# First gated features of the down projection loaded through the weights' rings in the last pair, with the A12 product behind the sixth product

## The chip, the cores and the metric

The program runs on one core of one Trainium2 chip. The metric is the device time of one execution in microseconds. The engines that matter here are TensorE (PE, matmuls), VectorE (DVE), ScalarE (ACT), GpSimd (POOL) and SyncE (SP), which issues all DMAs of this part of the program. Each engine works through its own instructions in program order; an instruction waits until the semaphores it needs have been raised.

## What is computed

Two layers of a hybrid block over 1024 latent tokens and 256 context tokens, each a mixing part and a channel part. The change lies in the channel part, which in both layers runs over the latent tokens with 1024 model features and 2816 hidden features:

```
def conv_ffn(h, w_up, w_conv, w_down):
    u = dwconv3(h @ w_up, w_conv)
    a, b = jnp.split(u, 2, -1)
    return (jax.nn.silu(a) * b) @ w_down

x = x + g2_x * rmsnorm(conv_ffn(hx, w_up[l], ffn_conv_w[l], w_down[l]), g_post_ffn[l])
```

`dwconv3` is a centred depthwise convolution of width 3 over the tokens. In layer 0 the context tokens take the same path afterwards.

## The kernel before

All matmuls are float32 products made of three: an operand is split into a high part (a rounded copy, `act.copy`, on ScalarE) and a low part (`dve.tensor_sub`, on VectorE), and high x high, high x low and low x high are summed.

**Up projection.** Hidden features go in 22 pairs `f` of 128 gate and 128 value features. The product of a pair, 256 features by 1024 tokens, is made as seven block products of half the size (`q1` to `q7`, 12 matmuls of 128 x 128 by 512 columns each), whose operands are sums and differences of the blocks of the weights and the tokens. `q2` is the product with the upper right block of the weights, A12, added in PSUM to `q1`'s result ("G"); `ev2` copies it out (L1191, ScalarE). `q7` and `q5` start the two halves of one PSUM tile "M2" (`cd`), `q5` ends with a copy of its half (L1204). `q6` goes to "M1"; when it is done, VectorE makes `v` (L1213) and `z` (L1214, from `v` and `q7`'s half). `q3` adds to the half that `q5` began, `q4` to that of `q7`; both write into the tile that `z` reads, and wait for `z`. On TensorE the order in a pair is `q7`, `q2`, `q5`, `q6`, `q3`, `q1` of the next pair, `q4`; the last pair has no `q1` behind it.

`gated(f)` then makes the pair's gated features: `z` and the copy of `q5` are joined (L1228), `cd` and `v` (L1226), `conv3` runs on both halves (L342 on ScalarE, L343 and L344 on VectorE), then SiLU (L1230), the product (L1232) and a write of the 128 x 1024 tile to DRAM, `gscr` (L1233). Its two tiles are from the pool "HC".

**Down projection.** When the last pair is done, the pools of the up projection close and the pool `dn` opens in their room. The tokens go in three groups of 384, 384 and 256. In each, the 22 tiles of gated features are worked off in steps of two (FG = 2; "group 0" is features 0 and 1 of the first token group, "group 1" features 2 and 3). For each feature a tile `gr` of the group's tokens is loaded from `gscr` (L1441), split into `gh` (L1443, ScalarE) and `gl` (L1444, VectorE), and multiplied with 128 rows of `w_down` (L1402 to L1404, in `down_into`). Matmuls of a group go by token tile, then by half of the output columns, then by feature: the third matmul of a group is the first that reads `gl` of its first feature, the sixth the first that reads `gl` of its second. Group 0 has 36 matmuls.

**Rings.** `weight()` loads a block into a "RAW" tile (3 buffers, L114) and splits it into "WH" and "WL" (4 buffers each; L118 on ScalarE, L119 on VectorE). The same three rings serve the up projection's weights (L1122, L1123 make their splits, and also those of the sums `s31` and `ss2`). `w_down` of features 0 and 1 (w0, w1) comes that way. `w_down` of features 2 to 9 stays resident: RAW (L1450), and a split into "H" tiles (L1452, L1453). A RAW buffer is free for the next load when its split is done.

**Beside it in layer 0.** After each group one step of the next layer's modulation runs: 1 MB of `w_mod` into an "HC" tile (L173) and 8 small matmuls (L184). And the norm of the two context tiles that come later is made early: loads of "T4" tiles (L1370), square and sum (L245, ScalarE), variance (L238, VectorE), a power (L239, GpSimd) and the scaling (L247, VectorE), once for each tile.

**What sets the order.** The program is recorded in the order of the source and then ordered anew, engine by engine, by a list scheduler with a cost for each instruction; an engine's order can thus differ from the source's. The rows of order below show what came out.

Of the kernel before, what the change touches and what calls it, by code (L numbers as in the profile page):

```python
# [6 lines left out]
F32 = mybir.dt.float32  # L7
F32R = mybir.dt.float32r
# [6 lines left out]
P = 128  # L15
# [9 lines left out]
FG = 2  # L25
# [3 lines left out]
def build(tc, d, out, dbg=None):  # L29
    nc = tc.nc  # L30
    act, dve, pool, pe, sp = nc.scalar, nc.vector, nc.gpsimd, nc.tensor, nc.sync
# [19 lines left out]
    gscr = [[dram.t([P, N], f"gscr{l}_{f}") for f in range(FF)] for l in range(DEPTH)]  # L51
# [22 lines left out]
    def M1():  # L74
        return cur["pool"].t([P, 512], "M1", cur["tags"]["M1"])
# [32 lines left out]
    def raw_tile():  # L108
        return wp.t([P, 1024], "RAW", 3)
# [768 lines left out]
    for l in range(DEPTH):  # L878
# [204 lines left out]
        def gate(s):  # L1083
            g = op.t([P, D], "gt", 1)
            gate_tile(m, 0, s, g)
            return g
# [7 lines left out]
        g, xn = None, []  # L1094
# [23 lines left out]
        def S():  # L1118
            return up_.t([P, 512], "S", 6)
# [6 lines left out]
        def wtiles():  # L1126
            return wp.t([P, 1024], "WH", 4, F32R), wp.t([P, 1024], "WL", 4, F32R)
# [57 lines left out]
        def q2(f):  # L1185
            blocks(pair[f]["a"], pair[f]["a1"], 1, b21, False)

        def ev2(f):
            w = pair[f]
            w["u"], w["w"] = hp_.t([P, 2, N], "HC", 2), hp_.t([P, 2, N], "HC", 2)  # L1190
            act.copy(w["u"][:, 0, 0:512], w["a"])  # L1191

        def q7(f, js=range(4)):
            w = pair[f]
            if js[0] == 0:
                w["cd"] = M2()
            blocks(w["cd"][:, 512:1024], w["s31"], 0, t3, True, js)
# [8 lines left out]
        def q6(f, js=range(4)):  # L1206
            w = pair[f]
            if js[0] == 0:
                w["b"] = M1()
            blocks(w["b"], w["ss2"], 1, t2, True, js)  # L1210
            if js[-1] == 3:
                w["v"], w["z"] = S(), S()
                dve.tensor_sub(w["v"], w["s1"], w["b"])  # L1213
                dve.tensor_add(w["z"], w["v"], w["cd"][:, 512:1024])  # L1214
# [28 lines left out]
        for i, t in enumerate(order):  # L1243
# [14 lines left out]
            if t == order[0] or t == 0:  # L1258
                g = gate(0 if t < NT else 1)
# [58 lines left out]
        for f in range(FF):  # L1318
            more = f + 1 < FF
            if f:  # L1320
                q7(f)
            if f and more:
                prep0(f + 1)
            if f > 1:
                q2(f)
            ev2(f)
            if f:
                q5(f)
                q6(f)
            if more:  # L1330
                prepa(f + 1)
                prepx(f + 1)
            if f:
                q3(f)
            if f and more:
                q1(f + 1)
            if more:
                prepy(f + 1)
            q4(f)
            gated(f)  # L1340
# [9 lines left out]
        dn = Pool(f"dn{l}", bufs=1, side="left")  # L1350
# [81 lines left out]
        for ts in ((0, 1, 2), (3, 4, 5), (6, 7)):  # L1432
            n0, n = P * ts[0], P * len(ts)
            pts = [M2() for _ in ts]
            xt = []
            for f0 in range(0, FF, FG):
                fs = range(f0, f0 + FG)
                g, w = {}, {}
                for f in fs:
                    gr = dn.t([P, n], "gr", 4)  # L1440
                    sp.dma_start(out=gr, in_=gscr[l][f][:, n0 : n0 + n])  # L1441
                    gh, gl = g[f] = dn.t([P, n], "gh", 6, F32R), dn.t([P, n], "gl", 6, F32R)
                    act.copy(gh, gr)  # L1443
                    dve.tensor_sub(gl, gr, gh.bitcast(F32))  # L1444
                    blk = d["w_down"][l, P * f : P * f + P, :]
                    if f in wd:
                        w[f] = wd[f]
                    elif FG <= f < FG + RES:
                        raw = raw_tile()
                        sp.dma_start(out=raw, in_=blk)  # L1450
                        h = H()
                        act.copy(h[:, 0], raw)  # L1452
                        dve.tensor_sub(h[:, 1], raw, h[:, 0].bitcast(F32))  # L1453
                        w[f] = wd[f] = h[:, 0], h[:, 1]
                    else:
                        w[f] = weight(blk)
                if f0 == FF - 3 * FG:
                    for t in ts:
                        x = dn.t([P, D], "x", 3)
                        sp.dma_start(out=x, in_=xmid[l][t])  # L1460
                        xt.append(x)
                for i, t in enumerate(ts):
                    for ns in halves:
                        for f in fs:
                            down_into(pts[i][:, ns], ns, g[f], w[f], slice(P * i, P * i + P), f == 0, f == FF - 1)
                    if f0 == FF - FG:
                        end_tile(t, pts[i], xt[i])
                for _ in range(4 if n0 == 0 else 2):
                    next(it2, None)
            if with_ctx and n0:  # L1470
                tkc = tkc or ctx_h2()
# [6 lines left out]
        if with_ctx:  # L1478
# [7 lines left out]
            g = {}  # L1486
# [124 lines left out]
```

## Time and profile before

| | us |
|---|---|
| median of 3 runs | 2774.09 (2771.47 to 2774.62) |
| profiled execution | 2772.39 |
| its span in the profile | 2770.5 |
| TensorE busy | 2677.6 (97%) |
| VectorE busy | 1712.1 (62%) |
| ScalarE busy | 1142.7 (41%) |
| GpSimd busy | 101.3 (4%) |

The mean granted clock of the execution is 0.99 of full. Busy time counts a matmul from its start to a modelled end, and matmuls overlap, so the share of TensorE doesn't tell how near it is to its peak. What is idle, and why, is read from the rows of single stretches.

### The profile page before, as it was taken

Reading aid. Unit: us, or ns where it says so; the run is one execution under the profiler, and the core shown is the slowest. Engines: PE = TensorE matmul, PEld = TensorE weight load, DVE = VectorE, ACT = ScalarE, POOL = GpSimd, SP = SyncE. Lnnn points to the kernel's source line nnn. Section 1 sums busy time; section 2 is a strip of 40 time slices with the busy share of each in tenths; the row PEclk is TensorE's granted clock in tenths of the full one; section 3 lists DMA queues with packets and bytes.
Section 4 is the critical chain, followed back from the end, with each engine's and each line's share of the span. In section 5 each row is a group of like instructions: output and inputs, shape, how many; then the busy total and the mean of one; then the engine's idle time right before and its main releaser. Section 6 shows DMA issues by size and latency. Waiting matters only on the chain. (4 is left out here: it accounts for less than half of the span.)

```text
span 2770.5 us, 36682 instructions
## 1 busy us (share of the span) xinstructions
PE 2677.6 (97%) x14096; PEld 2172.9 (78%) x14096; DVE 1712.1 (62%) x2917; ACT 1142.7 (41%) x1925; POOL 101.3 (4%) x142
## 2 busy tenths in 40 slices
PE   7999999999999997999999999999999999998998
PEld 4777888787788886777899877788777888886786
DVE  5445465547988887235577644465559888884434
ACT  5222345335544445224566512354455444443332
POOL 0002000010000000000000001100000000000000
PEclk9999999999999998999999999999999999999999
DMA  6631211453222225645565562322542222225534
GB/s 255 214 122 36 74 39 52 148 168 103 91 92 76 84 84 192 237 161 187 195 216 175 181 224 64 79 51 63 169 154 77 92 76 84 85 83 194 198 122 141
DMA packets 162902, 355.73 MB, mean 128 GB/s; under 512 B 49187, under 2 KB 90150, under 8 KB 156326
## 3 DMA queue, kind: packets, MB, share of 16 engines
q1 hardware_dynamic: 162726, 353.38, 38.6%
q8 instruction: 111, 1.82, 0.3%
q14 instruction: 65, 0.53, 0.1%
HBM read 292.74 MB, written 55.61 MB: 126 GB/s over the span
## 5 line engine op out<-in xcount | busy, mean ns | idle before, releaser
L119 DVE TENSOR_TENSOR WL<-RAW,WH 128x1024 fp32r<-128x1024 f32 x194 | 234.7, 1224 | 80.5 <-ACT WH L118 79.9
L118 ACT CAST WH<-RAW 128x1024 fp32r<-128x1024 f32 x194 | 200.4, 1048 | 138.0 <-PE G L310 79.7
L1402 PE MATMUL M<-WH,gh 128*128 128x512 f32 x536 | 216.8, 404 | 17.7 <-ACT gh L1443 15.3
L1444 DVE TENSOR_TENSOR gl<-gr,gh 128x384 fp32r<-128x384 f32 (+1 forms) x132 | 66.9, 511 | 253.9 <-ACT gh L1443 251.7
L1404 PE MATMUL M<-WH,gl 128*128 128x512 f32 x536 | 213.5, 399 | 1.9 <-DVE gl L1396 1.0
L1403 PE MATMUL M<-WL,gh 128*128 128x512 f32 x536 | 214.5, 400 | 0.0
L1443 ACT CAST gh<-gr 128x384 fp32r<-128x384 f32 (+1 forms) x132 | 62.3, 476 | 303.0 <-PE M L1403 292.7
L309 PE MATMUL G<-H,WH 128*128 128x512 f32 x384 | 153.1, 399 | 10.1 <-DVE nkl L695 6.2
L1174 PE MATMUL M<-H,WH 128*128 128x512 f32 x352 | 140.4, 402 | 16.4 <-ACT H L284 7.8
L1123 DVE TENSOR_TENSOR WL<-RAW,WH 128x1024 fp32r<-128x1024 f32 x88 | 107.6, 1223 | 77.5 <-ACT WH L1122 77.5
L310 PE MATMUL G<-H,WH 128*128 128x512 f32 x384 | 151.8, 395 | 0.0
L311 PE MATMUL G<-H,WL 128*128 128x512 f32 x384 | 151.6, 395 | 0.0
L1122 ACT CAST WH<-RAW 128x1024 fp32r<-128x1024 f32 x88 | 92.5, 1051 | 142.5 <-PE M L1175 78.6
L1175 PE MATMUL M<-H,WH 128*128 128x512 f32 x352 | 140.4, 399 | 0.7 <-DVE H L285 0.7
L310 PE MATMUL G<-HC,WH 128*128 128x256 f32 x496 | 141.0, 284 | 0.0
L1176 PE MATMUL M<-H,WL 128*128 128x512 f32 x352 | 139.7, 397 | 1.2 <-DVE WL L1123 1.2
L309 PE MATMUL G<-HC,WH 128*128 128x256 f32 x496 | 140.8, 284 | 0.1
L311 PE MATMUL G<-HC,WL 128*128 128x256 f32 x496 | 140.3, 283 | 0.0
L1174 PE MATMUL G<-H,WH 128*128 128x512 f32 x352 | 138.6, 394 | 1.4 <-ACT s L1183 1.4
L1174 PE MATMUL M<-HX,WH 128*128 128x512 f32 x352 | 139.4, 397 | 0.0
L1402 PEld LDWEIGHTS M<-WH,gh 128*128 128x128 f32 x536 | 102.2, 191 | 46.2 <-ACT gh L1443 17.0
L1176 PE MATMUL M<-HX,WL 128*128 128x512 f32 x352 | 138.2, 394 | 0.0
(395 smaller groups left out, 6933.2 us busy)
## 6 DMA issues: line engine op xcount, KB each, us to landing
RAW<-in_w_down SPq DMA_DIRECT2D x122, 512.0 KB, 4.2
RAW<-in_w_up SPq DMA_DIRECT2D x110, 512.0 KB, 3.5
mw<-in_w_mod SPq DMA_DIRECT2D x32, 1024.0 KB, 6.0
RAW<-in_w_in SPq DMA_DIRECT2D x44, 512.0 KB, 4.0
gscr<-HC SPq DMA_DIRECT2D x44, 512.0 KB, 2.6
gr<-gscr SPq DMA_DIRECT2D x88, 192.0 KB, 2.8
R<-in_w_up SPq DMA_DIRECT2D x22, 512.0 KB, 3.6
xmid<-x SPq DMA_DIRECT2D x18, 512.0 KB, 2.6
```

The source lines that it names most:

```text
L118: act.copy(hi, raw)
L119: dve.tensor_sub(lo, raw, hi.bitcast(F32))
L309: pe.matmul(o, hi[:, wk], tok.cols(k, 0, c), start=(k == 0), stop=False)
L310: pe.matmul(o, hi[:, wk], tok.cols(k, 1, c), start=False, stop=False)
L311: pe.matmul(o, lo[:, wk], tok.cols(k, 0, c), start=False, stop=(k == KT - 1))
L1123: dve.tensor_sub(lo, raw, hi.bitcast(F32))
L1174: pe.matmul(o, hi[:, wk], b.part(0, j), start=first, stop=False, skip_group_check=True)
L1175: pe.matmul(o, hi[:, wk], b.part(1, j), start=False, stop=False, skip_group_check=True)
L1176: pe.matmul(o, lo[:, wk], b.part(0, j), start=False, stop=last, skip_group_check=True)
L1402: pe.matmul(o, gh[:, tsl], hi[:, ns], start=start, stop=False)
L1403: pe.matmul(o, gh[:, tsl], lo[:, ns], start=False, stop=False)
L1404: pe.matmul(o, gl[:, tsl], hi[:, ns], start=False, stop=stop)
```

## The change

In the last pair (`more` is false) `q2` and `ev2` stand behind `q5` and `q6`, not ahead of them. Behind them the gated features 0 and 1 of the first token group are loaded, side by side, into one RAW tile (two DMAs of 192 KB) and split, 768 columns wide, into one WH and one WL tile (`gw`). Group 0 of the first token group takes its `gh` and `gl` from there instead of from `dn`. In each layer this makes one cast of 768 columns out of two of 384, and one subtraction out of two; the counts of matmuls and of DMAs stay.

```diff
--- before.py
+++ after.py
@@ -1321,12 +1321,24 @@
                 q7(f)
             if f and more:
                 prep0(f + 1)
-            if f > 1:
-                q2(f)
-            ev2(f)
+            if more:
+                if f > 1:
+                    q2(f)
+                ev2(f)
             if f:
                 q5(f)
                 q6(f)
+            if not more:
+
+                q2(f)
+                ev2(f)
+
+                g01 = raw_tile()
+                for i in range(FG):
+                    sp.dma_start(out=g01[:, 384 * i : 384 * i + 384], in_=gscr[l][i][:, 0:384])
+                gw = wtiles()
+                act.copy(gw[0][:, 0:768], g01[:, 0:768])
+                dve.tensor_sub(gw[1][:, 0:768], g01[:, 0:768], gw[0][:, 0:768].bitcast(F32))
             if more:
                 prepa(f + 1)
                 prepx(f + 1)
@@ -1437,11 +1449,14 @@
                 fs = range(f0, f0 + FG)
                 g, w = {}, {}
                 for f in fs:
-                    gr = dn.t([P, n], "gr", 4)
-                    sp.dma_start(out=gr, in_=gscr[l][f][:, n0 : n0 + n])
-                    gh, gl = g[f] = dn.t([P, n], "gh", 6, F32R), dn.t([P, n], "gl", 6, F32R)
-                    act.copy(gh, gr)
-                    dve.tensor_sub(gl, gr, gh.bitcast(F32))
+                    if n0 == 0 and f < FG:
+                        g[f] = [w_[:, n * f : n * f + n] for w_ in gw]
+                    else:
+                        gr = dn.t([P, n], "gr", 4)
+                        sp.dma_start(out=gr, in_=gscr[l][f][:, n0 : n0 + n])
+                        gh, gl = g[f] = dn.t([P, n], "gh", 6, F32R), dn.t([P, n], "gl", 6, F32R)
+                        act.copy(gh, gr)
+                        dve.tensor_sub(gl, gr, gh.bitcast(F32))
                     blk = d["w_down"][l, P * f : P * f + P, :]
                     if f in wd:
                         w[f] = wd[f]
```

The names in the rows of order are tiles with a running number; lines of the program after the change are up to 15 higher (L1338: the loads of `g01`, L1340 and L1341: its split; L1456, L1458, L1459: `gr`, `gh`, `gl`; L1465, L1467, L1468: the resident weights; L1382: T4). All rows are of layer 0. Layer 1 has the same moves up to the convolution; behind it stand, on VectorE, L1232 between the first and the second of four `gl`, before those of features 0 to 3 and after those of features 2 to 5.

VectorE, from the end of the convolution of the last but one pair to L1228 of the last pair; L1213 and L1214 are `v` and `z` of the last pair, WL_9200 is the low part of w1. Before:

```order
L119 TENSOR_TENSOR WL_9200<-RAW_9197,WH_9199 128x1024
L1232 TENSOR_TENSOR HC_8946<-HC_8946 128x1024
L1453 TENSOR_TENSOR H_9267<-RAW_9265,H_9267 128x1024
L1453 TENSOR_TENSOR H_9320<-RAW_9318,H_9320 128x1024
L1213 TENSOR_TENSOR S_9100<-s1_9014,M1_9087 128x512
L1214 TENSOR_TENSOR S_9101<-S_9100,M2_9045 128x512
L1453 TENSOR_TENSOR H_9331<-RAW_9329,H_9331 128x1024
L1228 TENSOR_TENSOR HC_9070<-S_9101,S_9085 128x512
```
After; WL_9189 is the low part of w0, WL_9195 that of w1:

```order
L119 TENSOR_TENSOR WL_9189<-RAW_9186,WH_9188 128x1024
L1232 TENSOR_TENSOR HC_8946<-HC_8946 128x1024
L1213 TENSOR_TENSOR S_9085<-s1_9014,M1_9072 128x512
L1468 TENSOR_TENSOR H_9251<-RAW_9249,H_9251 128x1024
L1214 TENSOR_TENSOR S_9086<-S_9085,M2_9045 128x512
L119 TENSOR_TENSOR WL_9195<-RAW_9192,WH_9194 128x1024
L1228 TENSOR_TENSOR HC_9101<-S_9086,S_9070 128x512
```
One H subtraction instead of two stands ahead of `z`; w0's split stands where w1's stood, and w1's comes behind `z`.

ScalarE, from the copy of `q5` of the last pair to the convolution's first steps and the cast behind them. Before:

```order
L1204 COPY S_9085<-M2_9045 128x512
L1452 CAST H_9331<-RAW_9329 128x1024
L1452 CAST H_9384<-RAW_9382 128x1024
L1452 CAST H_9395<-RAW_9393 128x1024
L1452 CAST H_9448<-RAW_9446 128x1024
L342 ACTIVATE HC_9071<-HC_9070,fcw_178 128x1024
L342 ACTIVATE HC_9071<-HC_9070,fcn_6150 128x1024
L1452 CAST H_9459<-RAW_9457 128x1024
```
After; WH_9194 is the high part of w1, L1191 is `ev2`:

```order
L1204 COPY S_9070<-M2_9045 128x512
L118 CAST WH_9194<-RAW_9192 128x1024
L1191 COPY HC_9101<-G_9001 128x512
L1467 CAST H_9262<-RAW_9260 128x1024
L1467 CAST H_9315<-RAW_9313 128x1024
L1467 CAST H_9326<-RAW_9324 128x1024
L1467 CAST H_9379<-RAW_9377 128x1024
L342 ACTIVATE HC_9102<-HC_9101,fcw_178 128x1024
L342 ACTIVATE HC_9102<-HC_9101,fcn_6150 128x1024
L1467 CAST H_9390<-RAW_9388 128x1024
```
Four casts of resident weights stand ahead of L342 in both; the numbers 9331 to 9448 belong to features 5 to 8, 9262 to 9379 to features 3 to 6.

VectorE, from the convolution's last step of the last pair on. Before:

```order
L344 SCALAR_TENSOR_TENSOR HC_9071<-HC_9070,fcn_6150,HC_9071 128x1023
L1453 TENSOR_TENSOR H_9459<-RAW_9457,H_9459 128x1024
L1232 TENSOR_TENSOR HC_9071<-HC_9071 128x1024
L119 TENSOR_TENSOR WL_9513<-RAW_9510,WH_9512 128x1024
L119 TENSOR_TENSOR WL_9525<-RAW_9522,WH_9524 128x1024
L1444 TENSOR_TENSOR gl_9182<-gr_9179,gh_9181 128x384
L238 TENSOR_SCALAR varp_10588<-ssp_10585 128x1
L1444 TENSOR_TENSOR gl_9194<-gr_9191,gh_9193 128x384
L247 TENSOR_SCALAR T4_10584<-T4_10582,rstdp_10587 128x1024
L238 TENSOR_SCALAR varp_10646<-ssp_10643 128x1
L247 TENSOR_SCALAR T4_10642<-T4_10640,rstdp_10645 128x1024
L1444 TENSOR_TENSOR gl_9251<-gr_9248,gh_9250 128x384
```
After:

```order
L344 SCALAR_TENSOR_TENSOR HC_9102<-HC_9101,fcn_6150,HC_9102 128x1023
L1468 TENSOR_TENSOR H_9390<-RAW_9388,H_9390 128x1024
L1232 TENSOR_TENSOR HC_9102<-HC_9102 128x1024
L1468 TENSOR_TENSOR H_9443<-RAW_9441,H_9443 128x1024
L1468 TENSOR_TENSOR H_9454<-RAW_9452,H_9454 128x1024
L238 TENSOR_SCALAR varp_10583<-ssp_10580 128x1
L247 TENSOR_SCALAR T4_10579<-T4_10577,rstdp_10582 128x1024
L238 TENSOR_SCALAR varp_10641<-ssp_10638 128x1
L247 TENSOR_SCALAR T4_10637<-T4_10635,rstdp_10640 128x1024
L1459 TENSOR_TENSOR gl_9246<-gr_9243,gh_9245 128x384
```
The splits of w0's and w1's successors and `gl` of features 0 and 1 are gone from here, two H subtractions have come, and `gl_9246` (feature 2) stands behind both L247 as `gl_9251` did.

SyncE, from the gate row's load to the gated tiles of the first groups. Before:

```order
L232 DMA gt_9174<-grow0_65 128x1024
L1441 DMA gr_9179<-gscr0_0_91 128x384
L1441 DMA gr_9191<-gscr0_1_92 128x384
L1233 DMA gscr0_21_112<-HC_9071 128x1024
L173 DMA HC_9239<-in_w_mod 128x2048
L173 DMA HC_9241<-in_w_mod 128x2048
L1441 DMA gr_9248<-gscr0_2_93 128x384
L1441 DMA gr_9259<-gscr0_3_94 128x384
L1441 DMA gr_9312<-gscr0_4_95 128x384
L1441 DMA gr_9323<-gscr0_5_96 128x384
```
After:

```order
L232 DMA gt_9181<-grow0_65 128x1024
L173 DMA HC_9234<-in_w_mod 128x2048
L1233 DMA gscr0_21_112<-HC_9102 128x1024
L1456 DMA gr_9243<-gscr0_2_93 128x384
L1456 DMA gr_9254<-gscr0_3_94 128x384
L1456 DMA gr_9307<-gscr0_4_95 128x384
L173 DMA HC_9236<-in_w_mod 128x2048
L173 DMA HC_9301<-in_w_mod 128x2048
L1456 DMA gr_9318<-gscr0_5_96 128x384
```
The two gated loads of group 0 are gone, one load of `w_mod` stands ahead of the write of the last pair's features (gscr0_21) and the other two behind the gated tile of feature 4.

## Rows read from the trace of the kernel before

A row of a timeline has the start in us, the time in us, engine, line, operation, tiles, size and count, and in brackets the idle time before it and what ended it.

**Rows 1.** The page's costliest groups: busy us, mean ns of one, idle before
```profile
L118 ACT CAST WH<-RAW 128x1024 fp32r<-128x1024 f32 x194 | 200.4, 1048 | 138.0 <-PE G L310 79.7
...
L1402 PE MATMUL M<-WH,gh 128*128 128x512 f32 x536 | 216.8, 404 | 17.7 <-ACT gh L1443 15.3
```

**Rows 2.** Timeline of TensorE, end of layer 0's up projection, groups 0 and 1
```profile
1075.40 0.75 PE L1174 MATMUL M<-H,WH 128*128 128x512 f32 x1 [2.80 <-DVE S L1214]
...
1093.21 0.79 PE L1402 MATMUL M<-WH,gh 128*128 128x512 f32 x1 [10.38 <-ACT gh L1443]
...
1104.93 0.40 PE L1404 MATMUL M<-WH,gl 128*128 128x512 f32 x1
...
1106.83 0.39 PE L1404 MATMUL M<-H,gl 128*128 128x512 f32 x1
```

**Rows 3.** Timeline of VectorE, same stretch; the last row is of layer 1
```profile
1070.47 1.22 DVE L1232 TENSOR_TENSOR HC<-HC 128x1024 f32<-128x1024 f32 x1
1071.61 2.35 DVE L1453 TENSOR_TENSOR H<-RAW,H 128x1024 fp32r<-128x1024 f32 x2
...
1088.94 1.28 DVE L344 SCALAR_TENSOR_TENSOR HC<-HC,fcn 128x1023 f32<-128x1023 f32 x1
...
1096.20 0.75 DVE L247 TENSOR_SCALAR T<-T,rstdp 128x1024 f32<-128x1024 f32 x1 [0.44 <-POOL rstdp L239]
...
1099.10 0.75 DVE L247 TENSOR_SCALAR T<-T,rstdp 128x1024 f32<-128x1024 f32 x1 [0.73 <-POOL rstdp L239]
...
2515.32 1.49 DVE L1444 TENSOR_TENSOR gl<-gr,gh 128x384 fp32r<-128x384 f32 x3
```

**Rows 4.** Timeline of ScalarE, same stretch; the last row is of layer 1
```profile
1084.17 1.15 ACT L342 ACTIVATE HC<-HC,fcw 128x1024 f32<-128x1024 f32 x1 [2.88 <-DVE HC L1226]
...
1102.45 1.56 ACT L1443 CAST gh<-gr 128x384 fp32r<-128x384 f32 x3 [4.26 <-DMA gr<-gscr]
...
2507.75 1.15 ACT L342 ACTIVATE HC<-HC,fcw 128x1024 f32<-128x1024 f32 x1 [2.59 <-DVE HC L1226]
```

**Rows 5.** Timeline of SyncE's DMA queue, layer 0 behind the last pair
```profile
1092.94 2.90 SPq L173 DMA_DIRECT2D HC<-in_w_mod  x2
1095.89 2.13 SPq L1441 DMA_DIRECT2D gr<-gscr  x4
```

**Rows 6.** Landing times of L1450, resident weights, 8 loads from 1050 to 1090
```profile
DMA to landing us min/median/max: 3.5/3.6/4.7
```

**Rows 7.** Landing times of L173, 8 loads of 1 MB from 1080 to 1180
```profile
DMA to landing us min/median/max: 4.7/5.4/6.9
```

**Rows 8.** The page's DMA issues: count, KB each, median us to landing
```profile
RAW<-in_w_down SPq DMA_DIRECT2D x122, 512.0 KB, 4.2
...
gr<-gscr SPq DMA_DIRECT2D x88, 192.0 KB, 2.8
```

**Rows 9.** Timeline of TensorE, end of layer 1's up projection, groups 0 and 1
```profile
2499.17 0.80 PE L1174 MATMUL M<-H,WH 128*128 128x512 f32 x1 [2.75 <-DVE S L1214]
...
2511.34 0.79 PE L1402 MATMUL M<-WH,gh 128*128 128x512 f32 x1 [4.93 <-ACT gh L1443]
...
2523.30 0.39 PE L1404 MATMUL M<-H,gl 128*128 128x512 f32 x1
```

**Rows 10.** Timeline of TensorE, first pairs of both layers, behind waits of 1.55 us
```profile
696.23 0.50 PE L1174 MATMUL M<-H,WH 128*128 128x512 f32 x1 [1.55 <-ACT WH L1122]
...
698.14 0.39 PE L1175 MATMUL M<-H,WH 128*128 128x512 f32 x1
...
2118.38 0.50 PE L1174 MATMUL M<-H,WH 128*128 128x512 f32 x1 [1.55 <-ACT WH L1122]
...
2120.57 0.63 PE L1175 MATMUL M<-H,WH 128*128 128x512 f32 x1
```

**Rows 11.** Windows: us, busy by engine (instructions), granted clock, DMA share, GB/s
```profile
1061.49:1072.61 11.12, 11.12 (x49) 8.82 (x47) 9.85 (x9) 7.16 (x8) 0.00 (x0) 1.00 0.35 110
...
1083.00:1093.21 10.21, 0.00 (x0) 0.00 (x0) 10.08 (x9) 7.57 (x10) 0.00 (x0) 0.63 0.79 290
```

## Prediction

> **What bounds the kernel now.** I read the page first, then TensorE's timeline around the end of each layer's up projection, then the timelines of the engine that ended each wait. On the page the first product of the down projection (L1402) has 17.7 us of idle time in front of it, 15.3 of them ended by the cast L1443 of a gated tile [rows 1]. The timeline shows where: in layer 0 TensorE stops twice, 2.80 us before the first matmul of q3 and 10.38 us before group 0 [rows 2]; in layer 1 it stops for 2.75 and 4.93 us [rows 9]. The rest of these stretches is TensorE's own time, partly at the lower of its two clock levels, 1.2 instead of 2.4 GHz. At full clock one matmul follows the other every 0.232 us (48 in 11.12 us [rows 11]). q3 and q4 are 24 matmuls, 23 steps, 5.35 us; from the first start to the last, which lies 0.4 before the next wait, they take 7.03 us in layer 0 and 6.84 in layer 1 [rows 2, 9], so 1.7 and 1.5 are lost to the clock after the waits of 2.80 and 2.75 us. Group 0 is 36 matmuls, 35 steps, 8.14 us, and takes 11.72 [rows 2]: 3.6 for the clock and short stops. In layer 1 from group 0's first to group 1's sixth are 41 steps, 9.53 us, and it takes 11.96 [rows 9]: 2.4 for the clock.
>
> That makes 20.9 us of waiting and 9.2 us of low clock and short stops, 30 us in all, at two places of each layer. The change goes for both places; the question is what is late next.
>
> **The wait of q3.** It was ended by z (L1214) [rows 2]. In front of z on VectorE stand, from 1070.47, L1232 (1.14), two H subtractions (2.35), then v and z until the wait's end near 1075.35 [rows 2, 3]. After the change one H subtraction stands there instead of two, which saves 1.13, and the whole row comes up to 0.4 us earlier, because ahead of the previous pair's convolution an H split and a weight split give way to one narrower split. z then ends near 1073.8 (1073.6 to 1074.2). TensorE's work up to that point is the same 48 matmuls in another order (q2 last), so it is done at the same 1072.6; the wait shrinks from 2.80 to 1.1 to 1.35 us and q3 starts 1.6 us earlier. The move of q2 adds no matmul. It lets q6 end 12 matmuls, 2.8 us, earlier, so that v can start as soon as L1232 is done, near 1071.2; with q2 in its old place v would wait for 1072.6, and z would end 0.4 to 1.4 later.
>
> Whether the clock falls after this shorter wait is open: a wait of 1.55 us was followed by full-speed matmuls (0.39) in one place and by matmuls at half speed (0.63) in another [rows 10]. I take it as kept; if it falls, q3 and q4 lose 1.5 again. Below, the end of group 0 sets nothing, so that this matters little.
>
> **Group 0.** Its gated tiles are in place long before: they are split in the previous pair's time on engines with room there, in exchange for two casts and two subtractions of 384 columns later. They cost TensorE nothing there. The casts of w0 and w1 now wait for slots of the WH ring that q5 and q2 free; both come free before q3 starts, and w1's split, two operations of 1.05 and 1.13, is done near 1075, 4 us ahead of group 0. In layer 0 q4 then ends near 1079.5, and group 0, 36 steps, near 1087.9 instead of 1105.2. In layer 1 q3 starts at 2497.5, q4 ends at 2503.1, group 0 at 2511.5 instead of 2522.
>
> **What is late next: group 1.** Its gated features 2 and 3 still go the old way, and the path to them has a new head. Resident weights now come one ring slot later, and four of their casts stand on ScalarE before the last convolution's first step L342 (four in both orders, but now of loads asked for later). The chain in layer 0: w0's split stands directly in front of L1232, which began at 1070.47 [rows 3]; 0.3 earlier it ends near 1070.2 and frees the slot; RAW_9260 lands L later; cast 1.05 [rows 1] and subtraction 1.2 free the slot of RAW_9377; that lands L later; its cast 1.05; then L342. So L342 starts at 1073.7 + 2L. For L this stretch shows 3.5 / 3.6 / 4.7 us (least, median, most) [rows 6], the page 4.2 over all loads [rows 8]; more loads now share the same time, so I take 4.2: 1082.1, against 1084.17 before [rows 4]. With 3.6 it is 1080.9, with 4.7 1083.1. It can't start before q4's last matmul lets L1226 through, near 1080.8.
>
> From L342 on, layer 0: the four convolution steps end 6.1 us later (1084.17 to 1090.2 [rows 3, 4]): 1088.2. VectorE then has an H subtraction, L1232 and two more H subtractions, 4 x 1.13: 1092.8. Two norm steps of the context stand ahead of gl of feature 2: variance, the power on GpSimd and L247, 1.7 (a wait of 0.73, then 0.75 [rows 3]); and ScalarE's L245 with the second variance, power and L247, whose start came 2.9 after the first L247's [rows 3], so 3.1 with the hand-over: 1097.6. Then gl, 0.5: 1098.1. That is L342 + 16, and it is the third matmul of group 1, which was at 1106.83 [rows 2]: 8.7 us earlier. The load for L184 is freed at L344's end, issued near 1088.4, and lands at most 6.9 later [rows 7], before 1095.3; the gated tile, asked for near 1092.1, lands by 1094.9 at the page's 2.8 [rows 8] and by 1096.4 at 4.3. So the norm steps end last. TensorE idles from 1087.9 to 1098.1 but for L184 and two matmuls, so the clock falls again; after q3's wait that cost 1.7, after the 10.38 us wait at most 3.6, but most of it now falls on L184 and the two matmuls before 1098.1. I take 1.2, between 0 and 1.7. **Layer 0 gains 7.5.**
>
> Layer 1 has no L184 and no norm steps. Up to L342 its chain is the same, 1423.8 us later by the starts of q3 in the two layers [rows 2, 9]: L342 = 2497.5 + 2L, 2505.9 at 4.2. gl of feature 3 stands directly behind L1232, where the gl at 2515.32 stood, 7.6 after L342 at 2507.75 [rows 3, 4]; with its own 0.5 and the hand-over 8.3: 2514.2. That is the sixth matmul of group 1, which was at 2523.30 [rows 9]: 9.1 earlier. TensorE stops twice there, for 0.5 us at the third matmul and some 1.2 at the sixth; for the clock I take 1.1 of the 1.5 that the 2.75 us wait cost. **Layer 1 gains 8.0.**
>
> The sum is 15.5 us: a span of 2755.0, a profiled run of 2756.9 against 2772.39, and a median 15.5 below 2774.09, **2758.6**. Bounds: with L = 3.6 in both layers and no clock lost 20 us, with L = 4.7 and the full 1.7 and 1.5 12.6 us. That is 2754 to 2761.5.
>
> **A rule against it.** In the trace, gated tiles that were issued at 1095.89 behind two 1 MB loads [rows 5] set ScalarE's cast off only at 1102.45 [rows 4], though the page's median is 2.8 us [rows 8]. The Trainium skill, "DMA: Bandwidth & Descriptors", section "Queues, rings and completion order", says that all transfers that SyncE issues share one row of rings, and that each DMA engine consumes them in ring order. By that rule the tile of feature 2 would come behind the 1 MB load for L184 and the 0.5 MB write of the last gated features: at 5.4 us per MB [rows 7] near 1097.5, gl at 1098.6 instead of 1098.1, and the median 2759.1. The trace agrees with the rule.
>
> **Rivals.** (A) Half the gain: loads land at 6 instead of 4.2 us. DMA engines are already busy 0.79 of the time between 1083 and 1093.21 [rows 11], and the change pulls all loads closer together. L342 comes 3.6 later in each layer, which leaves 15.5 - 7.2 = 8.3: 2765.8; with lower clock, 2769. For it speaks that share; against it the 4.7 that was the most in this stretch.
>
> (B) Nothing is late: group 1 follows group 0 without a wait. Then of the 30 us only q3's shorter waits stay, 2.5: 2746.6. Against it stands the convolution's length, 6.1 us after q4, and the norm steps.
>
> (C) Slower. The one mechanism is the chain of two loads in front of L342: before, the four casts waited for loads issued one slot earlier. Its price is 2 us per us of L in each layer; it breaks even where 1073.7 + 2L + 16 = 1106.83, L = 8.6, and 2497.5 + 2L + 8.3 = 2523.3, L = 8.75. At L = 10 layer 0 comes 2.9 later and layer 1 2.5: 2779.5. No load of resident weights in this stretch took over 4.7 [rows 6].
>
> (D) The change doesn't do what it says for q3: its wait stays as it was, because w0's split waits and holds up L1232 and z. Then q4 and group 0 end 1.6 later; in layer 0 that hides behind the norm steps, in layer 1 group 0 ends at 2513.1 and the sixth matmul still waits for gl. The time is 2758.6 to 2760, inside the forecast's range.
>
> **Chances.** The forecast with (D) 0.76, (A) 0.15, (B) 0.04, (C) 0.03, and 0.02 for loads between (A) and (C) that leave next to nothing. The bounds 2754 to 2761.5, a microsecond more below, and the nearer half of (A) give 2753 to 2767, which holds some 8 in 10. 0.2%, 5.5 us, is about what a measurement of this kernel can tell from no change. Faster by more, under 2768.5: the forecast, (B) and 0.12 of (A), 0.92; within: 0.03 of (A) and the 0.02, 0.05; slower: 0.03.
>
> **What would show it.** Right: q3's wait near 1.2 us and still ended by L1214; no wait between q4 and group 0; in layer 0 a wait of 4 to 10 us after group 0 that ends at a gl behind L247, in layer 1 of under 3 us ended by gl or gh. Wrong: a wait at group 0 for a WH or WL tile; L342 after 1084; w_down loads of 6 us; or group 1 starting at 1088.

## The result and the profile after

The changed kernel takes 2757.94 us (median of 4 runs, 2757.34 to 2758.56) against 2773.6 for the kernel before with one run more: a ratio of 0.9945, 95% interval 0.9933 to 0.9958, 15.7 us less. Measured again later beside other kernels it was 2759.93 against 2772.86, 0.9959 (0.9945 to 0.9973), 12.9 us less. The forecast was 2758.6, range 2753 to 2767.

The profiled execution took 2758.56 us, its span is 2756.4, 14.1 less than before. On the page the group that led the forecast's argument has all but lost its idle time, 1.9 us instead of 17.7 [rows 1] (group 0's first products, in front of which most of it lay, now stand in a group M<-WH of their own), while the gated tiles' landing became slower, 3.8 us instead of 2.8 [rows 8]:

```profile
L1414 PE MATMUL M<-WH,gh 128*128 128x512 f32 x512 | 204.3, 399 | 1.9 <-DVE y L1429 1.1
...
gr<-gscr SPq DMA_DIRECT2D x84, 192.0 KB, 3.8
```

TensorE's timeline in layer 0; start, time, and in brackets the idle time before. It answers to [rows 2]:

```profile
1073.85 0.50 PE L1174 MATMUL M<-H,WH 128*128 128x512 f32 x1 [1.05 <-DVE S L1214]
...
1079.50 0.39 PE L1414 MATMUL M<-WH 128*128 128x512 f32 x1
...
1087.43 0.39 PE L1416 MATMUL M<-WH,WL 128*128 128x512 f32 x1
1095.89 1.93 PE L184 MATMUL G<-HC,sc 128*32 128x512 f32 x8 [8.07 <-DMA HC<-in_w_mod]
1098.24 0.80 PE L1414 MATMUL M<-H,gh 128*128 128x512 f32 x1 [0.42 <-ACT gh L1458]
1098.83 0.63 PE L1415 MATMUL M<-H,gh 128*128 128x512 f32 x1
1099.26 0.63 PE L1416 MATMUL M<-H,gl 128*128 128x512 f32 x1
```

q3 waits 1.05 us and runs at full clock (a matmul every 0.23 us); group 0 follows q4 at once. Then TensorE stands 8.07 us ahead of L184, for its load, and 0.42 for gh of feature 2, and group 1 begins at half clock (a matmul every 0.43 us). In layer 1 (answering to [rows 9]):

```profile
2489.22 0.50 PE L1174 MATMUL M<-H,WH 128*128 128x512 f32 x1 [1.05 <-DVE S L1214]
...
2503.16 0.50 PE L1414 MATMUL M<-H,gh 128*128 128x512 f32 x1
...
2504.08 0.50 PE L1416 MATMUL M<-H,gl 128*128 128x512 f32 x1 [0.19 <-DVE gl L1459]
...
2507.54 0.50 PE L1416 MATMUL M<-H,gl 128*128 128x512 f32 x1 [2.50 <-DVE gl L1459]
```

**Where the 14.1 us are.** I laid both traces side by side, matmul by matmul. At q3's wait in layer 0 the new one is 0.2 us behind: q2 ends at 1072.80, where q6 of before ended at 1072.60. From there it gains 6.5 in layer 0, as the second modulation step shows, before and after (42.25 and 35.77 us behind those ends):

```profile
1114.85 1.07 PE L184 MATMUL G<-HC,sc 128*32 128x512 f32 x8
```

```profile
1108.57 1.07 PE L184 MATMUL G<-HC,sc 128*32 128x512 f32 x8
```

Between there and layer 1's last pair come 2.0 more, nearly all at one place in the context's channel part, where the profiled execution of before stopped twice:

```profile
1397.61 0.50 PE L1402 MATMUL M<-WH,gh 128*128 128x512 f32 x1 [0.51 <-ACT gh L1395]
...
1399.31 0.50 PE L1404 MATMUL M<-WH,gl 128*128 128x512 f32 x1 [0.97 <-DVE gl L1396]
```

Half clock followed there (a granted clock of 0.68 between 1400 and 1405). The execution of the changed kernel has one wait of 0.97 us at this place, its second execution below waits of 0.29 and 0.98, and both stay at 1.00; so most of these 2.0 belong to that one execution and not to the change. Layer 1 gains 5.85.

### The profile page after: what moved, and what is told of

Same layout as the page of the kernel before. It is cut to its first block, busy times and chain, and to the rows that moved or that the text cites. A ratio compares the mean times of both kernels' runs of the same rounds, so it can differ in the third digit from the quotient of the medians.

```text
span 2756.4 us, 36678 instructions
## 1 busy us (share of the span) xinstructions
PE 2672.5 (97%) x14096; PEld 2168.9 (79%) x14096; DVE 1711.2 (62%) x2915; ACT 1142.8 (41%) x1923; POOL 101.2 (4%) x142
## 4 chain that ended last, share of the span: by engine, by line
PE 76%; DVE 5%; DMA 2%; ACT 2%; issue 1%; POOL 0%; DVEq 0%; POOLq 0%; SPq 0%; ACTq 0%
PE M L1174 7%; PE M L1176 7%; PE M L1175 7%; PE M L1414 6%; PE M L1416 6%; PE M L1415 6%; PE G L309 4%; PE G L310 4%; PE G L311 4%; PE G L1174 3%; PE G L1176 3%; PE G L1175 3%; PE M L1062 2%; PE M L1063 2%; PE M L1061 2%
## 5 line engine op out<-in xcount | busy, mean ns | idle before, releaser
L1459 DVE TENSOR_TENSOR gl<-gr,gh 128x384 fp32r<-128x384 f32 (+1 forms) x128 | 64.6, 510 | 237.5 <-ACT gh L1458 235.7
L1414 PE MATMUL M<-WH,gh 128*128 128x512 f32 x512 | 204.3, 399 | 1.9 <-DVE y L1429 1.1
L1416 PE MATMUL M<-WH,gl 128*128 128x512 f32 x512 | 202.3, 395 | 1.0 <-DVE gl L1408 1.0
L1415 PE MATMUL M<-WL,gh 128*128 128x512 f32 x512 | 202.3, 395 | 0.0
L1458 ACT CAST gh<-gr 128x384 fp32r<-128x384 f32 (+1 forms) x128 | 60.6, 475 | 287.4 <-PE M L1415 273.2
L309 PE MATMUL G<-H,WH 128*128 128x512 f32 x384 | 153.0, 398 | 10.1 <-DVE nkl L695 6.1
L311 PE MATMUL G<-H,WL 128*128 128x512 f32 x384 | 151.6, 395 | 0.0
L1176 PE MATMUL G<-H,WL 128*128 128x512 f32 x352 | 137.9, 392 | 0.0
```

Source lines behind the costliest of these rows:

```text
L309: pe.matmul(o, hi[:, wk], tok.cols(k, 0, c), start=(k == 0), stop=False)
L311: pe.matmul(o, lo[:, wk], tok.cols(k, 0, c), start=False, stop=(k == KT - 1))
L1176: pe.matmul(o, lo[:, wk], b.part(0, j), start=False, stop=last, skip_group_check=True)
L1414: pe.matmul(o, gh[:, tsl], hi[:, ns], start=start, stop=False)
L1415: pe.matmul(o, gh[:, tsl], lo[:, ns], start=False, stop=False)
L1416: pe.matmul(o, gl[:, tsl], hi[:, ns], start=False, stop=stop)
```

## The experiments

The traces reach the last pair of layer 0 up to 4.7 us apart. Part of this are short waits earlier on that are followed by full clock in some executions and by half clock in others. Times of a trace are therefore compared by their distance from the end of q2 or q6 ahead of q3.

**The two halves of the change.** First the move of `q2` alone, in the kernel before:

```diff
-            if f > 1: q2(f)
-            ev2(f)
+            if more:
+                if f > 1: q2(f)
+                ev2(f)
             if f: q5(f); q6(f)
+            if not more: q2(f); ev2(f)
```

> The kernel before, with the move of q2 behind q6 in the last pair alone; the gated tiles come the old way. Theory 1 (each of the two waits has its own cause): z ends 1.1 us earlier, q3 waits about 1.6 instead of 2.8 us, the clock may stay up for q3 and q4; group 0 still waits for gh of feature 0, which follows from the last convolution, itself 1.1 to 2.8 us earlier. Gain 1.1 to 2.8 us per layer, 2 to 5.6 in all: 2768 to 2771.5 us. Rival (the move buys nothing, since group 0's wait takes back what q3 gains): 2773 to 2774.

Measured: 2770.47 us (10 runs), ratio 0.999 (0.998 to 1.0), 3.1 less than before, measured beside it. TensorE's timeline, layer 0:

```profile
1073.72 0.47 PE L1174 MATMUL M<-H,WH 128*128 128x512 f32 x1 [1.51 <-DVE S L1214]
...
1092.40 0.80 PE L1406 MATMUL M<-WH,gh 128*128 128x512 f32 x1 [12.88 <-ACT gh L1447]
```

q3's wait falls from 2.80 to 1.51 and the clock stays up, but group 0's wait grows from 10.38 to 12.88: 2.5 of the 2.9 us that q3's wait and clock give back are waited off again there. Since group 0 then loses less, 2.4 us remain in layer 0; in layer 1 0.2 remain. So theory 1's time holds, at the edge of what the interval can tell from nothing, and in layer 1 its rival's account is the right one.

Then the gated features alone, with `q2` where it was:

```diff
-            if more:
-                if f > 1: q2(f)
-                ev2(f)
+            if f > 1: q2(f)
+            ev2(f)
             if f: q5(f); q6(f)
-            if not more: q2(f); ev2(f)
```

> The changed kernel with q2 in its old place; only the gated features 0 and 1 come through the rings. Theory 1: v waits for q6 (1072.6) and stands behind the split of w1 and one H subtraction, z ends near 1075, q3 waits 2.4 us or more and the clock falls; group 0 still follows q4 without a wait; the last convolution starts 1 to 1.5 us later than in the changed kernel, and so does group 1, in each layer. 1 to 1.5 us per layer behind the changed kernel: 2760 to 2761 us. Rival (without the move the prefetch has no room and its split delays q3 by more): over 2764.

Measured: 2758.56 us, ratio 0.9945 (0.993 to 0.9959). That is 0.6 more than the changed kernel, 1.4 to 2.4 less than theory 1 had and far from its rival. q3 waited 2.43 us and ran at half clock, as expected, and group 0 came 2.8 us later; but the wait behind it was shorter, 5.87 us for L184 in layer 0 (8.07 and, in a second execution, 5.86 in the changed kernel), and in layer 1 there is only one of 0.20:

```profile
2512.27 0.50 PE L1411 MATMUL M<-H,gl 128*128 128x512 f32 x1 [0.20 <-DVE gl L1454]
2512.60 0.39 PE L1409 MATMUL M<-H,gh 128*128 128x512 f32 x1
```

Against the trace of before, layer 0 gains 6.1 us here and layer 1 7.6. So nearly the whole gain is the gated tiles'. By the traces the move adds 0.4 or 2.3 us in layer 0, for the two executions of the changed kernel, and costs 1.8 in layer 1; the times put it at a microsecond or so. What made layer 1 better without the move stays open.

**What group 1 waits for in layer 0.** The forecast said the norm steps. Two kernels: one has the first modulation step behind group 1, the other leaves out the norm.

```diff
-                for _ in range(4 if n0 == 0 else 2):
+                for _ in range((4 if f0 else 0) if n0 == 0 else 2):
```

> The changed kernel with the first modulation step of layer 0 behind group 1 instead of group 0, so that no 1 MB load stands ahead of the gated tiles of features 2 and 3 on SyncE; nothing is left out. Theory A (in layer 0 group 1 waits for the gated tile, which lands late behind the modulation load and the write of the last pair's features): the tile lands 4 us or less after it is asked for, before 1094, gl of feature 2 is then next behind three H subtractions, 1093.3 to 1094.6, and the third matmul of group 1 comes at 1094 to 1095 instead of 1099.3: 4 to 5 us faster, 2753 to 2754 us. Theory B (the norm steps of the context end last): gl of feature 2 stands ahead of both here, that of feature 3 between them, so the sixth matmul comes near 1094.5 too; the two don't differ by more than 0.5 us in this run.

> The kernel with the first modulation step behind group 1 once more, since its time (0.5 us less than the changed kernel) and its trace (some 4 us less by the middle of layer 0's down projection) did not agree. If the trace is right, 2753.5 to 2756 us; if the gain is given back later in each run, 2757 to 2758 us again, and the alignment of the two traces shows the place.

Measured: 2757.42 and, the second time, 2755.65 us; ratios 0.9939 (0.9924 to 0.9953) and 0.9943 (0.9927 to 0.996). The times can't tell this from the changed kernel. The traces can:

```profile
1093.78 0.60 PE L1414 MATMUL M<-H,gh 128*128 128x512 f32 x1 [4.39 <-ACT gh L1458]
...
1095.14 0.80 PE L1416 MATMUL M<-H,gl 128*128 128x512 f32 x1
```

From q3's start (1075.42) to the third matmul are 19.7 us instead of 25.4, in the second execution of the changed kernel 23.8. Of these 5.7, 1.1 are the step that now comes later; by the third token group the two executions are 4.1 and 4.3 us ahead of the changed kernel's first trace, 2.1 and 2.4 ahead of its second. It does not stand in the times in full: these executions had lost 1.6 and 2.4 us against the changed kernel's first trace ahead of q3 already. But the reason given was wrong: the tile came no faster, with no modulation load ahead of it. SyncE and ScalarE:

```profile
1086.64 0.91 SPq L1456 DMA_DIRECT2D gr<-gscr  x2
```

```profile
1093.22 0.94 ACT L1458 CAST gh<-gr 128x384 fp32r<-128x384 f32 x2 [1.53 <-DMA gr<-gscr]
```

The cast that waited for the tile starts 6.6 us after the tile was asked for. It came earlier since it was asked for earlier, ahead of the write of the last pair's features (1092.37). Theories A and B were not to be told apart by this run, since gl of feature 2 stands ahead of the norm steps in it.

```diff
-                xn = tpool.t([P, D], "T4", 3)
-                prenorm(x, xn)
+                xn = x
```

> The changed kernel without the norm of the two context tiles in front of the context's channel part (its square, variance, power and scaling are left out, so the context path computes something else); two modulation loads now stand ahead of the gated tile of feature 2. Theory A (the landing of the gated tile sets group 1 in layer 0): nothing gained, 0 to 2.5 us slower for the second 1 MB load: 2758 to 2760.5 us. Theory B (the norm steps set it): gl of feature 2 follows the H subtractions at 1093.3 and group 1 comes 4 to 5 us earlier: 2753 to 2754 us.

Measured: 2762.13 us (2758.43 to 2767.4), ratio 0.996 (0.9947 to 0.9973): slower by 4.2, where theory B had it 4 to 5 faster and theory A at most 2.5 slower. But it doesn't decide between the two, for the order on SyncE changed with the removal: the write of the last pair's features and both modulation loads, issued 1093.62 to 1096.65, now stand ahead of the gated tiles, and L184 is what waits in the profiled execution (2767.2 us, one of the two long ones):

```profile
1101.74 1.94 PE L184 MATMUL G<-HC,sc 128*32 128x512 f32 x8 [11.69 <-DMA HC<-in_w_mod]
```

**What a gated tile's landing hangs on.** The gate row's load (0.5 MB), which stood right ahead of the tiles in layer 1, is asked for later:

```diff
-        gate_tile(m, 1, 0, gt2)
...
                 if f0 == FF - 3 * FG:
+                    if n0 == 0: gate_tile(m, 1, 0, gt2)
```

> The changed kernel with the load of the gate row (0.5 MB, gt, needed only at the end of a token group) asked for 8 groups later; in layer 1 nothing else on SyncE moves, and the gated tiles of features 2 to 5 stand directly behind the weights. Theory D (a gated tile lands late by what was asked for ahead of it on SyncE's queue and is not yet moved, some 3.2 us per MB here): in layer 1 it lands 1.6 us earlier, 4.9 instead of 6.5 us after it is asked for; the casts, SiLU, L1232 and gl of feature 3 all move with it, and the wait at group 1's sixth matmul falls from 2.5 to about 1 us. In layer 0 the gate row is moved long before the tiles are asked for: 0 to 1 us. Together 1.5 to 3 us faster than the changed kernel. Rival (the tiles' landing has nothing to do with what is ahead of them): 6 us or more still, wait unchanged.

Measured: 2754.9 us, ratio 0.9938 (0.9924 to 0.9953). That is 3 to 5 us less than the changed kernel, but before, measured beside it, was faster too (2770.63): against that the gain is 15.7 us, for the changed kernel 15.7 and 12.9. The trace has the difference in layer 1, 10.1 us instead of 5.85. Landing times of the tiles in layer 1, for three of the four, and of the changed kernel's below, for two of four:

```profile
DMA to landing us min/median/max: 3.7/5.5/5.5
```

```profile
DMA to landing us min/median/max: 6.5/6.5/6.5
```

The first tile is some 2.6 us faster (3.7; in the changed kernel its cast starts 6.3 after it was asked for), the others 1.0: for the landing theory D has the cause and the order of size, though in the kernel before, with the gate row ahead as well, two of the tiles took 3.2 and 3.5. The 2.5 us wait at the sixth matmul is gone, and with it the half clock, 4.2 us for layer 1. This is not theory D's doing as it was told, for SiLU didn't move with the tiles: it starts 15.8 us after q3's start (2487.29), in the changed kernel 15.5. What changed is the order on VectorE, where gl of feature 3 now stands ahead of L1232, which waits for SiLU:

```profile
2501.65 1.02 DVE L1458 TENSOR_TENSOR gl<-gr,gh 128x384 fp32r<-128x384 f32 x2
...
2504.13 1.23 DVE L1232 TENSOR_TENSOR HC<-HC 128x1024 f32<-128x1024 f32 x1 [1.47 <-ACT HC L1230]
```

In layer 0 the tiles landed in 3.7 to 4.1 us (two of three), and here the norm steps do end last, VectorE and TensorE:

```profile
1097.03 0.75 DVE L247 TENSOR_SCALAR T<-T,rstdp 128x1024 f32<-128x1024 f32 x1 [0.73 <-POOL rstdp L239]
1097.70 1.49 DVE L1458 TENSOR_TENSOR gl<-gr,gh 128x384 fp32r<-128x384 f32 x3
```

```profile
1098.31 0.79 PE L1416 MATMUL M<-H,gl 128*128 128x512 f32 x1 [0.51 <-DVE gl L1458]
```

**SiLU behind the gated casts in layer 1.** Two instead of four buffers for loaded gated tiles:

```diff
-                        gr = dn.t([P, n], "gr", 4)
+                        gr = dn.t([P, n], "gr", 2)
```

> The changed kernel with two instead of four buffers for the loaded gated tiles. In layer 1 the casts of features 4 and 5 then stand behind L1230 and no longer ahead of it. Theory C (in layer 1 the sixth matmul of group 1 is late because SiLU of the last pair stands behind four gated casts that wait for their tiles, and L1232 and gl of feature 3 behind SiLU): L1230 starts 0.9 to 1.1 us earlier, the 2.5 us wait falls to about 1.5. Rival (the landing of the tiles sets it): unchanged, 2.5 us. Elsewhere two buffers may cost something in each group; the trace of this stretch decides, not the time: 2754 to 2765 us.

Measured: 2751.65 us, ratio 0.9922 (0.9908 to 0.9936), some 6 to 8 us less than the changed kernel. The wait at the sixth matmul fell to 1.44:

```profile
2499.46 1.05 ACT L1230 ACTIVATE HC<-HC 128x1024 f32<-128x1024 f32 x1
```

```profile
2502.30 0.50 PE L1416 MATMUL M<-H,gl 128*128 128x512 f32 x1 [1.44 <-DVE gl L1459]
```

SiLU starts 14.5 us after q3's start (2484.98) instead of 15.5; theory C holds. Layer 1 gains 8.4 us instead of 5.85. The larger part of the gain is in layer 0 and was not expected: the tiles of features 2 and 3 are asked for at 1081.30, far ahead of the modulation load, and no wait there is longer than 1.6 us.

**Both groups through the rings.** A second RAW, WH and WL tile brings features 2 and 3, once with the first modulation step behind group 1 and once behind group 0 as in the changed kernel:

```diff
+                for j in range(2):
                     g01 = raw_tile()
                     for i in range(FG):
-                        ... gscr[l][i][:, 0:384]
+                        ... gscr[l][FG * j + i][:, 0:384]
...
-                    if n0 == 0 and f < FG:
+                    if n0 == 0 and f < 2 * FG:
```

> The changed kernel with the gated features 2 and 3 brought in the same way (a second RAW, WH and WL tile), and the first modulation step of layer 0 behind group 1. Theory A (what is left after the change is the path of the gated tiles of group 1: write and modulation load ahead of them on SyncE, landing, cast, subtraction): z follows v at once and q3 waits under 0.4 us; group 0 and group 1 run without a wait, in layer 0 to about 1095.3; the modulation load, free about 1086.5, lands by 1093; group 2 waits at most 1 us. 11 to 12 us in layer 0 and 4 to 5.5 in layer 1 faster than the changed kernel: 2740.5 to 2743 us. Rival (the rings are the limit: with two gated tiles in them w1's split and the weights of features 3 to 5 come too late and TensorE waits for these instead): gain under 8 us, over 2750, with waits ended by L118, L119, L1471 or L1472.

> The kernel with two groups through the rings, but with the first modulation step of layer 0 behind group 0 as in the changed kernel. Theory E (in layer 0 two things stand ahead of group 1, the modulation load for L184 and the gated tile; taking away one alone leaves the other): L184 waits some 5 to 7 us for its load after group 0, the clock falls, then group 1 and 2 run through; layer 1 as with two groups. 6 to 9 us slower than with the step moved: 2746 to 2749 us. Rival (the modulation load is not what counts, the gated tile alone is): within 2 us of 2739.5.

Measured: 2739.49 us (2738.95 to 2742.2), ratio 0.9881 (0.9868 to 0.9895), with the step moved; 2743.4, ratio 0.9899 (0.9884 to 0.9914), without. The first is 18 to 20 us faster than the changed kernel and beats both. Theory A's mechanism holds and its gain was a little too small (18.6 us in layer 0 and 12.3 in layer 1 against the trace of before); the rings did not become the limit. Of all waits in both places one is left, in layer 0 at group 2:

```profile
1095.13 0.50 PE L1418 MATMUL M<-H,gh 128*128 128x512 f32 x1 [0.37 <-ACT gh L1462]
```

and the clock stays up (windows; us, busy by engine, granted clock, DMA share, GB/s):

```profile
1070.00:1079.00 9.00, 9.00 (x40) 7.18 (x39) 7.35 (x9) 4.88 (x6) 0.00 (x0) 1.00 0.69 221
1079.00:1096.00 17.00, 16.63 (x77) 12.63 (x76) 12.93 (x15) 9.61 (x13) 1.10 (x2) 1.00 0.83 298
```

Without the moved step L184 waits, but only 2.42 us, and the clock does not fall:

```profile
1093.13 1.07 PE L184 MATMUL G<-HC,sc 128*32 128x512 f32 x8 [2.42 <-DMA HC<-in_w_mod]
```

That is 3.9 us slower by the medians themselves, 5 by the ratios and 6.1 by the medians, each against before as measured beside it, where 6 to 9 were expected; 2.0 of it is in layer 0 by the traces. Theory E has the right obstacle, but a wait of 5 to 7 us and a fall of the clock were expected of it and did not come. The step stands 20 matmuls, 4.6 us, further back than expected, in the middle of group 1, and the last convolution starts earlier with two groups brought in (L342 7.1 us after q3's start, in the changed kernel 8.3), and with it the load.

The changed kernel itself ran once more beside these:

> The changed kernel once more, beside the two below on the same chip: 2757 to 2759 us, and in the trace q3's wait 1.05 us in both layers, 8 us for the modulation load ahead of group 1 in layer 0, 2.5 us at group 1's sixth matmul in layer 1.

Measured: 2759.93 us (2757.78 to 2764.21). q3's 1.05 and layer 1's 2.50 are the same; L184's wait is 5.86 instead of 8.07, and layer 0's stretch gains 8.4 us instead of 6.5, against the trace of before. So that stretch differs by 1.9 between two executions of one kernel, and the next section shows that it ends differently in them.

## Why the prediction was right, step by step

**q3's wait.** Forecast 1.1 to 1.35 us, ended by L1214, clock kept: measured 1.05, ended by L1214, clock kept, in both layers.

**Group 0.** Forecast from 1079.5 to 1087.9 in layer 0 without a wait; measured 1079.50 to 1087.8.

**L342 behind two loads.** Forecast 1073.7 + 2L with L = 4.2, 1082.1. ScalarE went from the fourth cast straight into L342 at 1082.14 (in [rows 4] it had idled 2.88 us there), and the loads took 3.6 to 4.4:

```profile
1081.18 1.05 ACT L1467 CAST H<-RAW 128x1024 fp32r<-128x1024 f32 x1 [0.72 <-DMA RAW<-in_w_down]
1082.14 1.15 ACT L342 ACTIVATE HC<-HC,fcw 128x1024 f32<-128x1024 f32 x1
```

Rival C's chain is thus real and sets L342, at half the length at which it would cost anything; rival A's loads of 6 us did not come.

**What is late next in layer 0: wrong in one execution, right in the other.** Forecast: the norm steps until 1097.6 and gl of feature 2 at 1098.1, the gated tile landed before 1096.4. Measured, SyncE, ScalarE and VectorE of the changed kernel, first execution:

```profile
1088.35 0.33 SPq L173 DMA_DIRECT2D HC<-in_w_mod  x1
1090.57 0.32 SPq L1233 DMA_DIRECT2D gscr<-HC  x1
1090.93 2.27 SPq L1456 DMA_DIRECT2D gr<-gscr  x3
```

```profile
1097.67 1.48 ACT L1458 CAST gh<-gr 128x384 fp32r<-128x384 f32 x3 [2.08 <-DMA gr<-gscr]
```

```profile
1096.51 0.75 DVE L247 TENSOR_SCALAR T<-T,rstdp 128x1024 f32<-128x1024 f32 x1 [0.73 <-POOL rstdp L239]
1098.22 1.53 DVE L1459 TENSOR_TENSOR gl<-gr,gh 128x384 fp32r<-128x384 f32 x3 [0.96 <-ACT gh L1458]
```

The norm steps end at 1097.3, 0.3 earlier than worked out; the tile, asked for at 1090.9, takes 6.7 us and is there at 1097.6. The step that failed here is the landing, "lands by 1094.9 at the page's 2.8 [rows 8] and by 1096.4 at 4.3": the page's median was carried to a place where the rows of the same place [rows 4, 5] already showed 6.5. The load for L184 ahead of it, forecast to land before 1095.3, released L184 only at 1095.9, 7.5 us after it was issued, where the most in [rows 7] was 6.9. The third matmul came at 1099.26 instead of 1098.1.

The second execution has the same order on SyncE, and there the tile landed in time; SyncE, the landing times of the three tiles, ScalarE, VectorE and TensorE:

```profile
1089.22 0.33 SPq L173 DMA_DIRECT2D HC<-in_w_mod  x1
...
1091.81 2.02 SPq L1456 DMA_DIRECT2D gr<-gscr  x3
```

```profile
DMA to landing us min/median/max: 4.1/4.6/4.6
```

```profile
1096.51 1.47 ACT L1458 CAST gh<-gr 128x384 fp32r<-128x384 f32 x3
```

```profile
1097.38 0.75 DVE L247 TENSOR_SCALAR T<-T,rstdp 128x1024 f32<-128x1024 f32 x1 [0.73 <-POOL rstdp L239]
1098.05 1.49 DVE L1459 TENSOR_TENSOR gl<-gr,gh 128x384 fp32r<-128x384 f32 x3
```

```profile
1098.66 0.80 PE L1416 MATMUL M<-H,gl 128*128 128x512 f32 x1 [0.36 <-DVE gl L1459]
```

The tile is there at 1096.4, the cast follows, and gl follows the second L247 at once: the norm steps end last, as forecast. The third matmul comes 23.8 us after q3's start; the forecast had 24.3 (1073.8 to 1098.1), the first execution 25.4. The kernel with the later gate row shows the same chain, with 24.1. So the chain of norm steps was worked out well, and it and the tile end within 2 us of each other: which of them is last differs from execution to execution. The tile's landing was taken too short and as one number.

The Trainium skill, "DMA: Bandwidth & Descriptors", section "Queues, rings and completion order", says that SyncE's transfers have one row of rings and that each DMA engine consumes descriptors in ring order; by it the forecast had put the landing at 1097.5 and gl at 1098.6. The first trace agrees, with 1097.6 and 1098.7; in the second, where q3 starts 1.0 later, the tile landed sooner, at 1096.4. In both it landed 1.7 us behind L184's start, which waits for the 1 MB load ahead of it. That load released L184 7.5 us after its issue in one execution and 5.5 in the other; why it did is open.

Layer 0 gained 6.5 and 8.4 us in the two executions; 7.5 were forecast.

**Layer 1: a term left out.** Forecast: the sixth matmul 9.1 us earlier, 1.1 back for the clock. Measured 5.85 for the layer. With the 8.25 us by which this execution was ahead there, 2507.54 answers to 2515.8 of before instead of 2514.2. The missing 1.6 is the order on ScalarE: SiLU stands behind four gated casts, and these waited for the tile (landing 6.5 us; the second execution has the same 2.50 us wait):

```profile
2502.59 2.21 ACT L1458 CAST gh<-gr 128x384 fp32r<-128x384 f32 x4 [2.32 <-DMA gr<-gscr]
2504.71 1.05 ACT L1230 ACTIVATE HC<-HC 128x1024 f32<-128x1024 f32 x1
```

The forecast placed gl of feature 3 by its distance from L342 before, when the tiles were there in time: SiLU then started 4.95 us after L342, here 7.57. That wait of the casts, and of SiLU behind them, is the term put at nothing. For the clock the forecast took 1.1; the matmuls at half clock behind the 2.5 us wait lost some 1.7.

**The sum.** 15.5 was forecast, 7.5 and 8.0. The two places gave 6.5 and 5.85 us in one trace, 8.4 and 5.84 in the other, 12.3 and 14.2 in all; the medians differ by 15.7 and 12.9. So layer 0's amount was right on the average of the two, layer 1 was taken too high by some 2 us, and that the first measurement came out within 0.7 of the forecast is in part luck: it holds more than the two places gave in its own trace.

## What to carry to other kernels

When a wait is taken away, follow the next consumer on every engine that feeds it, and on the queue above all: what stands ahead of its load there, in bytes, and which other work stands behind the instruction that waits for it. A landing time belongs to its place; take it from rows of the same stretch and not from a median over the program, and as a range. Before one execution is said to show which of two chains ends last, take a second one. And a prefetch that moves one group's wait to the next group is half done: with the second group brought in the same way the gain about doubled, from 13 to 16 us to 27, and to 33 with the modulation step moved.

## What the runs showed that I had not expected

The same tiles of 192 KB, behind the same loads on SyncE, landed in 6.1 to 6.7 us in one execution of the changed kernel and in 4.1 to 4.6 in another, while the page's median is 2.8 or 3.8. Taking a piece of work away (the norm) made the kernel 4 us slower by the median, with another order on SyncE. And the same two short waits, 1.55 and 0.61 us near 696 us, far from any change, stand in all twelve traces; full clock followed in six, among them before [rows 10] and the first execution of the changed kernel, and half clock in the other six, among them its second execution:

```profile
695.91 0.50 PE L1174 MATMUL M<-H,WH 128*128 128x512 f32 x1 [1.55 <-ACT WH L1122]
...
698.20 0.63 PE L1176 MATMUL M<-H,WL 128*128 128x512 f32 x1
```

The granted clock between 699 and 701 us is 0.50 in it, 1.00 in the first; this alone cost it 1.2 us. Single executions thus differ by 1 to 4 us at places that the change does not touch, which is as much as some of the effects above.
